# Reordering TensorE work inside the steps of the RWKV stage: side pieces before the projections instead of between two halves of them

## The chip, the cores and the metric

The kernel runs on one core of a Trainium2 chip. The metric is the device time of one execution in microseconds (us), as a median of several runs. One profiled execution gives the trace that is read here.

## The reference, cut to what matters

One decoder layer with two head groups of 8 heads x 64 over 1024 tokens of width 1024, all in float32. The normalised input goes through one wide input projection. Group A is sparse attention. Group B is the RWKV-7 recurrence, whose state depends on the token before:

```
h = rms_norm(x);  proj = h @ w_in          # columns for both groups
state, sa = 0, ...
for t in tokens:                            # per head, 64 x 64 state
    sa    = state @ (-kk_t)
    state = state * w_t + sa (x) (kk_t * a_t) + v_t (x) k_t
    y_t   = state @ r_t
y = group_norm(y) * gn_w + gn_b + bonus
out = rms_norm(x + concat(attention, y * gate) @ w_out)
```

## The kernel before, in words

The recurrence is computed in chunks of 64 tokens. The 1024 tokens x 8 heads are cut into 8 units (n = 0 to 7): a unit is two pairs of heads over 256 tokens, that is 4 chunks. Inside a chunk the recurrence is a triangular system, so a unit needs preparation (its **side work**) and then a **chain** of 12 dependent steps, three for each chunk (`wkv_chain`). A chain step is a burst of 8 small float32 matmuls in two groups into the PSUM tiles `pc` and `py`, and a copy of the result by VectorE (`z`, or `x1` at L682 and L689) and ScalarE (L683, L690). The next step's burst reads those copies.

`weave(n, ...)` runs the 12 steps of unit n. After each burst it puts other TensorE work, so that TensorE has something to do while the copies are made:

- **projections** (`filler.step`): matmuls of the input projection, 128x128 by 128x512 in fp32r, into tiles `p_...`, 48 to a group of 128 columns. Each step takes a quota of 7 or 8 of them (7 for n = 0, 1, 2, 6, 7; 8 for n = 3, 4, 5). The weights of the next group are fetched by DMA and split in two parts by ScalarE and VectorE (L342, L344) at fixed places within the group before (tiles `gn2r`, `gn2h`, `gn2l`, for example).
- **side pieces** (`piece(gen)`): generators that prepare later units or finish earlier ones. `sides` says at which of the 12 steps j each yields its next piece:
  - `wkv_values(n+1)`: transposes `pbt` (j = 0) and `pvt` (j = 1)
  - `wkv_elementwise(n+2)`: `pss` (first piece, at j = 11 of the unit before), `pw` (j = 1), `pa_` (2), `pn` (3), VectorE, ScalarE and GpSimd work at 4 and 5 (GpSimd L514, L522; VectorE L525), `pbon` (8)
  - `wkv_products(n+2)`: `pp` (j = 6 and 7), masked copies `g` (L555), then a DMA round trip `g` -> `dA` -> `la`, and from j = 10 through j = 5 of the next unit 31 rounds of two dependent GpSimd operations (L584, L586), which invert the triangles; the result goes through `dT` to `tt`
  - `wkv_inverse(n+1)`: VectorE transpose of `tt` (L633, j = 9), `px` (10), `pt` (11)
  - `wkv_norm(n-1)`: `pvar` (0), VectorE (2), `pyn` (4)
  - for n = 6 and 7 also `rotate` and `compress` (tiles `pcm`, weights `w`).

TensorE and GpSimd execute in the order in which the program is written (`manual_schedule(engines={PE, Pool})`). For VectorE, ScalarE and SyncE (which issues all DMAs, L85) a scheduler orders the instructions when the kernel is built: the chain has the highest priority, then the side pieces, then the projections' own copies and splits. `piece` adds that a side piece's VectorE and ScalarE instructions queue behind the chain's last copy on their engine (`gate`, `issue_after`); that is an order of issue, not a wait for completion.

A step of 12 that has no side piece on TensorE (j = 5 and 9, mostly) runs its whole quota of projections in one go already.

Of the kernel before, what the change touches and what calls it, by code (L numbers as in the profile page):

```python
# [74 lines left out]
def trunk_kernel(ctx, tc, x, norm_g, w_in, cmp_pos_k, cmp_w1_k, cmp_w2_k, cmp_pos_v, cmp_w1_v,  # L75
# [1143 lines left out]
    def g_gn(r):  # L1219
# [6 lines left out]
    filler = Filler([groups[n] for n in  # L1226
                     ("wda k0 k1 r0 r1 v0 v1 r2 k2 r3 k3 v2 v3 kc0 kc1 ks kw q0 q1 q2 q3 "
                      "gn1 gn0 gn2 gn3 gr0 gr1 gr2 gr3").split()])
# [4 lines left out]
    def piece(gen):  # L1233
        with ExitStack() as s_:
            s_.enter_context(tc.high_priority(offset=100000))
            for ins in gate.values():
                s_.enter_context(tc.issue_after(ins.ins))
            return next(gen, None)

    def whole(gen):  # L1240
        with tc.high_priority(offset=100000):
            for _ in gen:
                pass

    def weave(n, sides, quota):


        chain = wkv_chain(n)
        for j in range(12):
            with tc.high_priority(offset=200000):  # L1250
                next(chain)
            filler.step(quota // 2)
            for gen in sides.get(j, ()):
                piece(gen)
            filler.step(quota - quota // 2)
        whole(chain)

    TRI, EDGE, TRI_T, EDGE_T = range(4)
# [44 lines left out]
    with tc.manual_schedule(engines={E.PE, E.Pool}):  # L1303
# [7 lines left out]
        for n in range(8):  # L1311
# [43 lines left out]
            if n == 7:  # L1355
                nxt(1, 0, 1, 2, 3, 4, 5)
                side(call(lambda: begin(compress(1, cmp_w1_v, cmp_w2_v))), 3)
                nxt(2, 6, 7, 8, 9, 10, 11)
            weave(n, sides, (7, 7, 7, 8, 8, 8, 7, 7)[n])
        for g in keys:  # L1360
            assert next(g, None) is None
# [177 lines left out]
```

## Time and profile before

| what | value |
|---|---|
| three timed runs | 1038.44, 1043.26, 1045.9 us; median 1043.26 us |
| the profiled execution | 1040.26 us, of which the trace spans 1038.5 us |
| TensorE busy (matmuls) | 930.2 us, 90% of the span |
| VectorE, ScalarE, GpSimd busy | 584.0, 335.5, 448.2 us |
| mean granted TensorE clock | 0.951 of 2.4 GHz |
| the eight weaves (n = 0 to 7) | from 196.8 to about 581 us of the span |

PE is TensorE's matmuls, PEld its weight loads, DVE VectorE, ACT ScalarE, POOL GpSimd, SPq the queue on SyncE that issues DMAs. A matmul row's duration is modelled and overlaps the next; the distance from one start to the next is what TensorE really takes for it. "idle before <-X" is the time that the engine stood still ahead of an instruction, and what ended it.

### The profile page before, as it was taken

What the parts mean: (1) busy time and instruction counts of PE and PEld (TensorE: products, weight loads), DVE (VectorE), ACT (ScalarE), POOL (GpSimd) and SP (SyncE); (2) the same over time, 40 slices, a digit from 0 to 9 for tenths busy, and PEclk for the clock granted to TensorE, in tenths of its full rate; (3) what the DMA queues carried; (4) which work ended last, traced back from release to release, by engine and by line L of the source; (5) the groups of instructions that cost most, each with busy time, mean ns of one, the idle gap of its engine ahead of it and who ended that gap; (6) DMA issues with size and microseconds to landing.
All of it is one profiled execution on the core that took longest, in us unless ns stands there. A gap on an engine that the chain in (4) does not pass through costs nothing.

```text
span 1038.5 us, 17087 instructions
## 1 busy us (share of the span) xinstructions
PE 930.2 (90%) x6353; PEld 658.6 (63%) x6353; DVE 584.0 (56%) x1245; ACT 335.5 (32%) x650; POOL 448.2 (43%) x732
## 2 busy tenths in 40 slices
PE   5999999989998999899669978689999999889976
PEld 4888777766676766677458756354565656455555
DVE  7533545555575657374424335677659856685544
ACT  5533233224233443243121212433333333224321
POOL 3100153466483847444521120577463555246521
PEclk9999999999999999799889988879999999899989
DMA  7433453424426453536476293741132312231121
GB/s 259 125 102 102 125 157 108 130 76 116 135 76 172 134 154 119 131 106 170 116 218 192 65 203 95 212 122 31 41 63 79 77 46 69 53 80 33 39 84 41
DMA packets 154429, 115.66 MB, mean 111 GB/s; under 512 B 54369, under 2 KB 132266, under 8 KB 154346
## 3 DMA queue, kind: packets, MB, share of 16 engines
q1 hardware_dynamic: 154346, 114.57, 40.3%
q8 instruction: 50, 0.82, 0.3%
q14 instruction: 33, 0.27, 0.1%
HBM read 76.19 MB, written 35.19 MB: 107 GB/s over the span
## 4 chain that ended last, share of the span: by engine, by line
PE 60%; DVE 10%; DMA 9%; POOL 7%; SPq 6%; issue 5%; ACT 2%; POOLq 0%; DVEq 0%; ACTq 0%
PE pout L113 7%; SPq L85 6%; PE pst L113 6%; PE po L113 5%; PE p_r L113 4%; PE p_k L113 3%; PE p_gn L113 3%; PE p_gr L113 3%; PE p_q L113 3%; PE pc L113 2%; POOL lt L586 2%; POOL ltmp L584 2%; PE ps L113 2%; PE pd L113 2%; PE pcm L113 2%
## 5 line engine op out<-in xcount | busy, mean ns | idle before, releaser
L584 POOL TENSOR_TENSOR ltmp<-la,lt 128x60 f32<-128x60 f32 (+24 forms) x248 | 83.7, 337 | 65.3 <-DMA la<-dA 42.7
L1042 ACT ACTIVATE prob<-pst 128x512 f32<-128x512 f32 x132 | 74.6, 593 | 109.9 <-PE pst L113 106.3
L1055 POOL TENSOR_TENSOR acc<-acc,prob 128x1024 f32<-128x1024 f32 x36 | 86.7, 2409 | 45.1 <-ACT prob L1042 44.9
L586 POOL TENSOR_TENSOR lt<-lt,ltmp 128x60 f32<-128x60 f32 (+24 forms) x248 | 87.6, 353 | 18.8
L113 PE MATMUL pst<-q,k 128*128 128x512 f32 (+1 forms) x264 | 82.3, 430 | 0.0
L994 DVE TENSOR_REDUCE bm<-ps 128x6 f32<-128x384 f32 (+1 forms) x106 | 63.5, 613 | 26.6 <-PE ps L113 26.0
L113 PE MATMUL po<-prob,vt 128*64 128x512 f32 x264 | 75.1, 648 | 0.0
L1055 POOL TENSOR_TENSOR acc<-prob 128x1024 f32<-128x1024 f32 x14 | 33.7, 2410 | 82.6 <-ACT prob L1042 82.6
L113 PEld LDWEIGHTS pst<-q,k 128*128 128x128 f32 (+1 forms) x264 | 48.9, 196 | 14.9 <-issue 5.7
L113 PE MATMUL pout<-woh,mh 128*128 128x512 f32 x128 | 57.6, 450 | 0.2 <-DVE xt L1153 0.2
L113 PE MATMUL ps<-k,q 128*128 128x384 f32 (+3 forms) x136 | 45.4, 386 | 7.7 <-DVE bm L994 3.7
L113 PE MATMUL pout<-wol,mh 128*128 128x512 f32 x128 | 51.3, 401 | 0.0
L113 PE MATMUL pout<-woh,ml 128*128 128x512 f32 x128 | 51.2, 400 | 0.0
L113 PEld LDWEIGHTS ps<-k,q 128*128 128x128 f32 x136 | 25.6, 205 | 35.2 <-DVE bm L994 14.3
L982 DVE TENSOR_REDUCE bm<-pd 128x8 f32<-128x512 f32 x40 | 27.4, 688 | 26.2 <-PE pd L113 26.0
L113 PEld LDWEIGHTS pout<-woh,mh 128*128 128x128 f32 x128 | 25.1, 196 | 20.7 <-issue 17.8
L683 ACT ACTIVATE x<-pc 64x128 f32<-64x128 f32 x32 | 8.7, 272 | 75.4 <-DVE x L682 75.2
L113 PE MATMUL pd<-k,q 128*128 128x128 f32 x160 | 31.1, 321 | 2.1 <-POOL k L868 2.1
L1077 POOL TENSOR_TENSOR wide<-rr,ones 128x512 f32<-128x512 f32 x16 | 17.1, 1068 | 36.1 <-DVE rr L1073 34.1
L1069 DVE TENSOR_REDUCE zz<-pz 128x4 f32<-128x512 f32 x32 | 21.8, 684 | 13.4 <-PE pz L1067 13.0
L1153 DVE TENSOR_TENSOR xt<-pout,xt 128x512 f32<-128x512 f32 x16 | 11.1, 691 | 32.4 <-PE pout L113 32.4
L113 PEld LDWEIGHTS pd<-k,q 128*128 128x128 f32 x160 | 25.9, 204 | 4.0 <-POOL k L868 2.4
(518 smaller groups left out, 2447.7 us busy)
## 6 DMA issues: line engine op xcount, KB each, us to landing
dM<-mix SPq DMA_DIRECT2D x24, 256.0 KB
q<-dQH SPq DMA_DIRECT2D x22, 256.0 KB
la<-dA SPq DMA_DIRECT2D x32, 128.0 KB
xt<-in_x_dram SPq DMA_DIRECT2D x8, 512.0 KB
out_dram<-xt SPq DMA_DIRECT2D x16, 256.0 KB
x<-in_x_dram SPq DMA_DIRECT2D x7, 512.0 KB
mixk<-dM SPq DMA_DIRECT2D x8, 256.0 KB
mixr<-dM SPq DMA_DIRECT2D x8, 256.0 KB
```

Source lines behind the costliest of these rows:

```text
L85: return nc.sync.dma_start(plain(o), plain(i))
L113: return T.matmul(o, l, r, start=start, stop=stop)
L584: G.tensor_tensor(tv, la[:, j:j + 1, j + 1:].to_broadcast([128, m, n]), lt[:, :m, j:j + 1].to_broadcast([128, m, n]), op=OP.mult)
L586: G.tensor_tensor(lt[:, :m, j + 1:], lt[:, :m, j + 1:], tv, op=OP.add)
L683: gate["A"] = A.activation(x1[1][HP[1], c:8:4, :], pv[HP[1], :, 64:128], AF.Copy)
L982: V.tensor_reduce(bm[:, g * 4:g * 4 + 4, j:j + 2], p.rearrange("p (r b c) -> p r b c", b=2, c=64), axis=AX.X, op=OP.max)
L994: V.tensor_reduce(bm[:, h0:h0 + n, j:j + 2 * w], p[:, :n * w * 128].rearrange("p (h b c) -> p h b c", h=n, c=64), axis=AX.X, op=OP.max)
L1042: A.activation(pr[:, g * 512:(g + 1) * 512], p, AF.Exp)
L1055: G.tensor_tensor(s, self.acc, pr, op=OP.add)
L1069: V.tensor_reduce(zz[:, g, :], p.rearrange("p (r k) -> p r k", r=4), axis=AX.X, op=OP.add)
L1077: G.tensor_tensor(wide, rr.rearrange("p r g -> p (r g)").unsqueeze(2).to_broadcast([128, 8, 64]), ones64.unsqueeze(1).to_broadcast([128, 8 ...
L1153: V.tensor_tensor(xt[:, hs], p, xt[:, hs], op=OP.add)
```

## The change

Within a step, the first half of the quota of projections moves from before the side pieces to behind them, so that all of a step's projections follow each other. The number of projections in a step, the side pieces and their steps stay as they are.

```diff
@@ -1249,10 +1249,9 @@
         for j in range(12):
             with tc.high_priority(offset=200000):
                 next(chain)
-            filler.step(quota // 2)
             for gen in sides.get(j, ()):
                 piece(gen)
-            filler.step(quota - quota // 2)
+            filler.step(quota)
         whole(chain)
```

## Rows read from the trace of the kernel before

**Rows 1.** Busy time by engine in unit n = 1, 3, 6 (stretch, length, busy, PEclk).

```profile
241.70:287.20 45.50, 43.16 (x457) 30.95 (x456) 25.82 (x66) 15.16 (x34) 27.92 (x73) 0.98 0.42 113
334.30:380.80 46.50, 45.49 (x453) 32.83 (x452) 28.05 (x69) 18.02 (x38) 28.12 (x69) 0.99 0.54 155
480.80:527.60 46.80, 37.80 (x401) 27.05 (x400) 22.52 (x42) 12.94 (x27) 30.97 (x63) 0.89 0.49 138
```

**Rows 2.** Timeline of PE, unit 1, steps 4 and 5 (start, duration, instruction).

```profile
259.01 0.50 PE L113 MATMUL p_kc<-hl,kc0h 128*128 128x512 f32 x1
...
259.81 0.60 PE L720 MATMUL pyn<-ident,nq 128*128 128x128 f32 x4
260.16 0.48 PE L113 MATMUL p_kc<-hl,kc0h 128*128 128x512 f32 x1
...
261.27 0.45 PE L113 MATMUL pc<-x,bt 128*64 128x64 f32 x8
...
261.88 0.50 PE L113 MATMUL p_kc<-hh,kc0h 128*128 128x512 f32 x1
...
263.70 0.45 PE L113 MATMUL pc<-x,g 128*64 128x64 f32 x8
```

**Rows 3.** Timeline of PE, unit 2, step 7: the three projections ahead of `pp`.

```profile
313.68 0.50 PE L113 MATMUL p_ks<-hl,ksh 128*128 128x512 f32 x1
...
314.58 1.16 PE L113 MATMUL pp<-ar,bk 64*128 64x128 f32 x16
```

**Rows 4.** Waits of PE from 196.8 to 581 us (total us, times, longest).

```profile
PE pcm L113 <- DMA w<-in_cmp_w_k_dram: 8.0, 1, 8.0
PE pss L113 <- ACT s L467: 5.9, 4, 2.1
PE p_gn L113 <- DVE gn2l L344: 4.9, 1, 4.9
PE p_gn L113 <- ACT gn2h L342: 4.1, 1, 4.1
PE pc L113 <- ACT x L683: 3.6, 2, 3.2
PE pp L113 <- DVE bk L525: 3.0, 4, 1.0
PE px L113 <- DVE t L633: 1.4, 3, 0.6
```

**Rows 5.** Timeline of all engines, unit 1, step 11.

```profile
281.78 0.40 PE L113 MATMUL py<-g,x 128*64 128x64 f32 x8
...
282.23 0.60 ACT L697 ACTIVATE nq<-py 128x512 f32<-128x512 f32 x1 [0.97 <-PE py L113]
...
283.88 0.90 ACT L467 ACTIVATE s<-mixk,cols 128x256 f32<-128x256 f32 x2
...
284.44 1.05 PE L113 MATMUL pss<-mi,s 128*128 128x2 f32 x8 [1.36 <-ACT s L467]
```

**Rows 6.** Timeline from 284.9 to 331.7 us: one turn of the triangles' rounds (POOL, SP, DVE, PE).

```profile
284.93 0.24 POOL L584 TENSOR_TENSOR ltmp<-la,lt 128x31 f32<-128x31 f32 x1 [5.50 <-DMA dKC<-kca]
...
308.56 1.46 POOL L522 TENSOR_TENSOR s<-s,mixk 128x512 f32<-128x512 f32 x1
...
310.05 0.75 DVE L525 TENSOR_TENSOR bk<-s,s 128x512 f32<-128x512 f32 x1 [1.17 <-POOL s L522]
...
310.85 1.16 PE L113 MATMUL pp<-ar,bk 64*128 64x128 f32 x16 [0.63 <-DVE bk L525]
...
315.54 2.56 SPq L85 DMA_DIRECT2D dT<-lt  x4
...
326.69 2.15 SPq L85 DMA_DIRECT2D la<-dA  x4
...
331.69 0.24 POOL L584 TENSOR_TENSOR ltmp<-la,lt 128x31 f32<-128x31 f32 x1 [7.83 <-DMA la<-dA]
```

**Rows 7.** Busy time and PEclk around a wait of unit 2's last step.

```profile
328.70:332.10 3.40, 1.47 (x38) 1.45 (x40) 0.48 (x3) 1.90 (x5) 0.33 (x2) 1.00 0.84 232
332.20:335.50 3.30, 3.30 (x28) 2.19 (x21) 1.27 (x5) 0.00 (x0) 2.52 (x11) 0.50 0.93 304
```

**Rows 8.** Timeline of DVE, then PE, unit 4, step 10, and PEclk behind it.

```profile
424.56 0.69 DVE L344 TENSOR_TENSOR q3l<-q3r,q3h 128x512 fp32r<-128x512 f32 x1 [5.05 <-ACT q3h L342]
425.17 0.28 DVE L682 COPY x<-pc 64x128 f32<-64x128 f32 x1
...
425.86 0.69 PE L113 MATMUL pc<-x,bt 128*64 128x64 f32 x8 [3.17 <-ACT x L683]
...
424.40:437.90 13.50, 10.92 (x84) 8.14 (x84) 4.72 (x18) 4.88 (x12) 9.04 (x29) 0.50 0.61 165
```

## Prediction

> **What bounds the kernel now.** I read the busy time by unit first, then the timeline of TensorE step by step, then its waits, and last the timeline of the engine that ends the recurring wait.
>
> By unit, TensorE is nearly full where no long wait falls: 43.16 of 45.50 us in unit 1 and 45.49 of 46.50 in unit 3, against 28 us for VectorE and for GpSimd [rows 1]. So a reader would expect a saving on TensorE to shorten the stage. The waits correct this. Most of TensorE's idle time is in a few long waits for DMA-fed data (`pcm` 8.0 us, `gn2l` and `gn2h` 4.9 and 4.1, `x` 3.2), and the recurring ones are two: `pss` for ScalarE, 5.9 us in 4 times, and `pp` for L525, 3.0 us in 4 times [rows 4]. The second is the important one, for what stands behind it is a loop that hardly contains TensorE. GpSimd begins the 31 rounds at 284.93 us when `la` has landed, works without a gap to L522 at 308.56, VectorE's L525 follows at 310.05 and `pp` starts at 310.85, having waited; the rounds' result leaves as `dT` at 315.54, `tt` and `dA` follow it in SyncE's queue, `la` is issued at 326.69 and lands for the next L584 at 331.69 [rows 6]. That turn takes 46.76 us, as long as the unit (287.2 to 334.3). `pp` showed such a wait in units 0, 1, 2 and 4 (4 times in rows 4). So as far as unit 4's step 6, at about 406 us, the stage goes by GpSimd and the DMA round trip, with TensorE close behind; from there to 581 us by TensorE and the long waits.
>
> **What the change removes.** One break in the run of projections. Three projections ahead of `pyn` take 0.80 us (259.01 to 259.81) and the four behind it 1.11 (260.16 to 261.27), 1.91 together; seven in one run take 1.82 (261.88 to 263.70) [rows 2]. So a step whose first side piece is a full-height one like `pyn` saves 0.09 us. Ahead of a half-height piece the three take 0.90 (313.68 to 314.58) [rows 3], and such a step saves 0.90 + 1.11 - 1.82 = 0.19 us. By the timeline 74 of the 96 steps carry a side piece on TensorE: 35 begin with a half-height one (`pbt` 7, `pvt` 7, `pp` 12, `px` 7, `pt` 2), 39 with a full-height one (`pyn` 7, `pa_` 6, `pbon` 6, `pss` 5, `pn` 5, `pcm` 8, `pw` 1, `pvar` 1). What a side piece costs directly behind the burst the trace shows too rarely to price; its first weight load may wait there for the burst, as it does not behind projections in the full-height case. I take 0 to 0.09 us saved in those 39, and 0.19 in the 35: 6.7 to 10.2 us of TensorE's time over the stage.
>
> The Trainium skill (TensorE: Matmul & The Clock Gate, Part 2, on loading the stationary operand) says that TensorE pulls weight loads ahead of matmuls still running. Taken alone that would make a break free and the saving zero; rows 2 and 3 show 0.09 and 0.19 us, and the measurement decides.
>
> **What the change adds.** The three or four projections that stood between burst and side piece were cover. Any side piece whose input comes later than the burst's end now bares that much more idle time: 0.80 to 0.90 us with a quota of 7, about 1.1 with 8 (four at the pitch of rows 2).
>
> - `pss` (units 0 to 4, step 11). The burst's last group starts at 281.78; ScalarE then does L697, the copy, L699 and L467, from 282.23 to past 284.4, and `pss` starts at 284.44 after 1.36 us of idle time [rows 5]. ScalarE's work does not move, since it follows the burst, so `pss` starts at the same distance and the idle time grows by 0.80. Three times 0.80 in units 0 to 2, 1.1 in unit 4, 0 to 1.1 in unit 3, where it did not wait: 3.5 to 4.6 us.
> - The first `pp` (units 0 to 5). Where it waited already it waits 0.9 longer (three times) or 1.1 (unit 4); 0 to 1.1 in units 3 and 5: 3.8 to 6.0 us.
> - `pcm` once, for its weights: 0.8. `px` once or more: 0.6 was its longest wait, 0.9 more.
> - The pieces that follow one another from step to step (`pbt` to `pvt`, `pw` to `pa_`, `px` to `pt`, `pp` to `pp`) shift together, so their distance stays a step: nothing.
>
> Together 9.0 to 12.3 us bared, against 6.7 to 10.2 saved. **If TensorE bound everything**, that would be -1.2 to +5.6 us. Behind a waiting side piece stand the projections and the next burst, in TensorE's own order; nobody else waits for them soon, as the chain's copies are then long made.
>
> **Where it falls.** Up to 406 us neither counts much. The loop of rows 6 holds TensorE in one step, between the two `pp` pieces, which come 0.2 us closer; and `dA` stands in SyncE's queue behind `tt`, which waits for GpSimd and not for `pp`. So `pp` of units 0 to 4 starts where it did, give or take: 0, with bounds of -1 (0.2 five times) and +2 (a DMA issued ahead of `la`). GpSimd's order is unchanged, since projections have almost no GpSimd work.
>
> From there on TensorE counts again:
>
> - unit 4, step 6: `pp` at the same time, but eight projections behind it instead of four: +0.9
> - steps left with a break removed: 12 half-height (2, 6 and 4 in units 4, 5, 6) at -0.19, so -2.3; some 17 full-height at -0.09 to 0, I take -0.05, so -0.8
> - bared: `pss` of unit 4 +1.1, `pp` of unit 5 +1.0 (L525 ended just ahead of it), `pcm` +0.8, so +2.9
>
> Sum: +0.7 us. The attention stage, from 581 us, is as before. The profiled execution took 1040.3 us, so 1041 by its account; the median of the runs lies 3.0 above it, and I forecast on that basis: 1043.3 + 0.7 = **1044 us**, no measurable change. About 1% (10.4 us) is what a measurement of this kernel can tell from none.
>
> **The rivals.**
>
> *Longer idle times cost clock (slower).* The rows show it once plainly: between 328.70 and 332.10 TensorE was busy 1.47 of 3.40 us at the full granted clock, 2.4 GHz, and in the next 3.30 us the grant was 0.50, that is 1.2 GHz [rows 7]. With half the rate, 3.3 us at that level lose some 1.6. The change makes five waits at `pss` (to 2.2 us and more) and four to six at `pp` (to about 1.6) longer. If each of some nine of them brings such a stretch, that is 15 us; GpSimd's loop hides part in units 0 to 3, though TensorE's slack there is only the idle time at `pp`. With the +0.7 and 60 to 90% of the 15 uncovered it gives 1053 to 1058 us; it decides from six such stretches in all. Against it: `pss` waited 1.36 us in unit 1 and the clock of that unit was 0.98 all the same [rows 1, 5]. The skill's page on TensorE (Part 1, the clock gate) states the same rule, that idle time lowers the clock and that gaps should be avoided; it speaks against this change. The trace agrees in rows 7.
>
> *The saving comes through and queues sort themselves out (faster).* In unit 4 the chain's copy L682 stood on VectorE behind a weight split that waited for its DMA; TensorE waited 3.17 us and then ran at 0.50 for 13.5 us, which lost about half of that [rows 8]. With side work out of VectorE's way earlier in each step, or with another order from the scheduler, this could vanish: -3.2 - 6.7, with 6.7 to 10.2 saved and only half of the bared time: about -13, 1030 us. Against it: the wait is for a fetch, which the change does not move ahead.
>
> *Another order on SyncE, VectorE and ScalarE.* The scheduler lays these queues out anew. The waits for `gn2` (9.0 us) and `w` (8.0) hang on the place of one DMA among others [rows 4]; either may shrink or grow by several us, of either sign. This widens the forecast's own range to 1036 to 1052.
>
> **How the numbers follow.** Forecast 0.66; clock and bared waits 0.20; saving and queues 0.14. The likeliest gives 1044. To leave out no more than 2 in 10 the range takes in part of both others: 1034 to 1056. Faster by over 1% (under 1032.8) 0.12, slower by over 1% (above 1053.7) 0.20, within 0.68.
>
> **What would show it.** Right: runs of seven take 1.82 us everywhere; `pss` idles 2.1 us or more in units 0 to 2 and `pp` 1.5; GpSimd's first L584 of each unit comes at the old distance (44 to 48 us). Wrong: GpSimd's turn shortens by more than 1 us, or idles for `pp`; PEclk of units 0 to 4 falls under 0.9; or one of the waits for `gn2`, `w` or `q3` changes by over 5 us, which would swamp the rest.

## The result, and the profile after

| | before | after |
|---|---|---|
| median of 6 runs each on one chip | 1042.72 us (1038.44 to 1045.9) | 1053.13 us (1051.47 to 1059.15) |
| span of the profiled execution | 1038.5 us | 1050.3 us |
| mean granted TensorE clock | 0.951 | 0.940 |

The ratio is 1.0106 [1.0072, 1.0141]: slower, by 10.4 us, on the border of what the prediction set as measurable (1%). The time lies within its range and 9 us above its point. The ratios, here and below, leave out executions over 1.5% slower than the fastest of their kernel and weigh all the others, so they can differ from the quotient of the medians by some 0.15%.

The first window of [rows 1], with unit 0 ahead of it (units 0 and 1 of the changed kernel: length, then busy us of PE, PEld, DVE, ACT, POOL, then PEclk, DMA share, GB/s):

```profile
154.70:248.40 93.70, 84.17 (x716) 64.33 (x715) 45.63 (x91) 26.37 (x55) 44.87 (x124) 0.96 0.41 109
248.40:295.40 47.00, 42.50 (x436) 31.74 (x434) 28.21 (x68) 15.65 (x35) 29.30 (x74) 0.94 0.40 112
```

Waits of PE in the changed kernel, as [rows 4] (total us, times, longest):

```profile
PE pss L113 <- ACT s L467: 10.5, 5, 3.4
PE pcm L113 <- DMA w<-in_cmp_w_k_dram: 9.4, 1, 9.4
PE pp L113 <- DVE bk L525: 7.8, 5, 4.2
PE p_gn L113 <- ACT gn2h L342: 4.7, 1, 4.7
PE p_gn L113 <- DVE gn2l L344: 3.9, 1, 3.9
```

In total the bared waits came as forecast: `pss` +4.6 us, `pp` +4.8, `pcm` +1.4; the waits for `gn2` stayed within 1 us of before. But they don't say where the time went. For that the trace is cut at fixed instructions: VectorE's first copy `z` of each unit, and the first matmul into `pst`, with which the attention stage begins. Both kernels were profiled a second time, for one execution alone shows what recurs no better than what doesn't. All are differences of start times in the traces, in us:

| | up to unit 0 | unit 0 | units 1 to 6 | unit 7 to first `pst` | from `pst` to the end | span |
|---|---|---|---|---|---|---|
| before | 153.5 | 89.0 | 285.7 | 92.7 | 417.6 | 1038.5 |
| before, again | 156.8 | 88.9 | 288.3 | 95.3 | 418.4 | 1047.6 |
| after | 154.7 | 93.7 | 287.5 | 92.5 | 421.8 | 1050.3 |
| after, again | 157.0 | 93.1 | 288.3 | 90.5 | 423.7 | 1052.6 |

By the means of the pairs: unit 0 +4.4 us, units 1 to 6 +0.9, unit 7 and behind -2.5, attention +4.8, start +0.7; together the 8.4 by which the mean spans differ (1051.45 and 1043.05). Only unit 0 and the attention stand clear of the scatter between two executions of one kernel. The stage as a whole, from the first `z` to the first `pst`, does not: 467.4 and 472.5 us before, 473.8 and 471.8 after. The change reorders the steps of unit 0 as of every unit; in the attention stage it touches not a line.

**Unit 0.** First SyncE's queue before, then that of the changed kernel, where `lc` are the masks for the attention and `v3r` is a weight fetch that waits for its buffer:

```profile
194.87 1.18 SPq L85 DMA_DIRECT2D lc<-in_late_dram  x2
...
199.01 0.38 SPq L85 DMA_DIRECT2D v3r<-in_w_in_dram  x1
```

```profile
199.87 0.38 SPq L85 DMA_DIRECT2D v3r<-in_w_in_dram  x1
200.30 1.34 SPq L85 DMA_DIRECT2D lc<-in_late_dram  x2
```

The scheduler put `lc` behind `v3r`; counted from the unit's first `z` it is issued 4.2 us later (200.30 - 154.7 against 194.87 - 153.5). GpSimd's order in unit 0 changed too. The rounds that run there and the casts of the masks (L1272; L1273 before) are written ahead of the `manual_schedule` block, and there GpSimd does not keep the program's order, other than the section on the kernel before has it. In the traces of before the two casts stand behind 6 begun rounds, L514 behind 14 and L522 behind 22; in both traces of after the casts stand behind 8 and 9, L514 behind 13 and L522 behind 20. From unit 1 on both kernels have L514 behind 20 and L522 behind 24. GpSimd in unit 0, first before, then after (the round behind L522 is the 23rd, of 54 columns, or the 21st, of 66):

```profile
195.90 0.24 POOL L584 TENSOR_TENSOR ltmp<-la,lt 128x31 f32<-128x31 f32 x1 [5.72 <-DMA la<-dA]
...
217.18 1.28 POOL L522 TENSOR_TENSOR s<-s,mixk 128x512 f32<-128x512 f32 x1
...
218.54 0.79 POOL L584 TENSOR_TENSOR ltmp<-la,lt 128x54 f32<-128x54 f32 x1
...
240.29 0.24 POOL L584 TENSOR_TENSOR ltmp<-la,lt 128x31 f32<-128x31 f32 x1 [6.35 <-DMA la<-dA]
```

```profile
196.83 0.24 POOL L584 TENSOR_TENSOR ltmp<-la,lt 128x31 f32<-128x31 f32 x1 [5.46 <-DMA la<-dA]
...
204.68 0.61 POOL L1272 CAST maskb<-lc 128x512 bf16<-128x512 f32 x1 [2.13 <-DMA lc<-in_late_dram]
...
219.37 1.26 POOL L522 TENSOR_TENSOR s<-s,mixk 128x512 f32<-128x512 f32 x1
...
220.71 0.80 POOL L584 TENSOR_TENSOR ltmp<-la,lt 128x66 f32<-128x66 f32 x1
...
244.36 0.24 POOL L584 TENSOR_TENSOR ltmp<-la,lt 128x31 f32<-128x31 f32 x1 [8.01 <-DMA la<-dA]
```

TensorE of the changed kernel:

```profile
216.75 0.45 PE L113 MATMUL py<-ar,x 64*64 64x64 f32 x8
221.40 2.08 PE L113 MATMUL pp<-ar,bk 64*128 64x128 f32 x16 [4.21 <-DVE bk L525]
...
225.76 0.45 PE L113 MATMUL pc<-z,tt 64*64 64x64 f32 x8
```

The same step before, and then the windows behind `pp` (PEclk is the third number from the end), before, after and in the second profile of after:

```profile
217.27 0.45 PE L113 MATMUL py<-ar,x 64*64 64x64 f32 x8
...
219.24 1.16 PE L113 MATMUL pp<-ar,bk 64*128 64x128 f32 x16 [0.62 <-DVE bk L525]
...
221.45 0.45 PE L113 MATMUL pc<-z,tt 64*64 64x64 f32 x8
```

```profile
219.20:221.40 2.20, 2.16 (x20) 1.64 (x20) 2.20 (x5) 0.24 (x1) 1.81 (x6) 1.00 0.49 137
```

```profile
221.30:225.70 4.40, 4.30 (x23) 3.46 (x23) 2.23 (x5) 0.22 (x1) 3.47 (x12) 0.62 0.58 179
```

```profile
223.90:228.30 4.40, 4.40 (x22) 3.69 (x23) 2.13 (x4) 0.00 (x0) 3.46 (x13) 0.50 0.58 179
```

From the unit's first `z`, TensorE reaches this burst 1.7 us earlier than before (216.75 - 154.7 against 217.27 - 153.5): the saving of the steps ahead is real. But GpSimd stands 2.13 us for `lc`, and L522 comes 1.0 us later, though two rounds fewer stand ahead of it; L525 ends later and `pp` starts 1.0 us later, so TensorE stands for 4.21 us instead of 0.62. Behind that wait it runs near 1.2 GHz: `pp` and its seven projections take 4.36 us where `pp` and four took 2.21, and three projections in a long run are worth 0.8 (three of seven in 1.81), so by this estimate 1.4 us are the clock's. GpSimd's turn is 47.5 us (45.8 in the second profile), before 44.4 and 44.3.

**The attention.** VectorE in its second tile, first before, then after:

```profile
698.00 0.19 DVE L930 SCALAR_TENSOR_TENSOR im<-imh,im 128x32 f32<-128x32 f32 x1
698.23 0.20 DVE L931 TENSOR_TENSOR im<-im,keep 128x32 f32<-128x32 f32 x1
...
700.37 0.69 DVE L1093 TENSOR_TENSOR t<-t,pos 128x512 f32<-128x512 f32 x1
```

```profile
706.21 0.94 DVE L930 SCALAR_TENSOR_TENSOR im<-imh,im 128x32 f32<-128x32 f32 x1
707.18 2.29 DVE L931 TENSOR_TENSOR im<-im,keep 128x32 f32<-128x32 f32 x1
...
711.42 2.22 DVE L1093 TENSOR_TENSOR t<-t,pos 128x512 f32<-128x512 f32 x1
```

GpSimd beside them, first before, then after:

```profile
695.10 2.80 POOL L1114 TENSOR_TENSOR wol<-wor,woh 128x1024 fp32r<-128x1024 f32 x1
700.51 2.79 POOL L1055 TENSOR_TENSOR acc<-acc,prob 128x1024 f32<-128x1024 f32 x1 [2.61 <-ACT prob L1042]
```

```profile
706.06 1.04 POOL L1077 TENSOR_TENSOR wide<-rr,ones 128x512 f32<-128x512 f32 x1
707.06 2.37 POOL L1114 TENSOR_TENSOR wol<-wor,woh 128x1024 fp32r<-128x1024 f32 x1
710.75 2.34 POOL L1055 TENSOR_TENSOR acc<-acc,prob 128x1024 f32<-128x1024 f32 x1 [1.32 <-ACT prob L1042]
```

Before, all three small operations begin in a gap of GpSimd (697.90 to 700.51). After, each begins while a GpSimd operation runs, and the first two end when those end (707.15 and 707.10; 709.47 and 709.43). They take 5.45 us instead of 1.08. `bm` (L994), for which TensorE waits, stands behind them on VectorE. Here the order on GpSimd is the scheduler's, and it put a weight split (`wol`) elsewhere.

All of the stage's loss can be seen to arise here: from this L930 to the next L1009 on VectorE it is 9.2 us in both traces of before and 14.1 in both of after, and from there to the third tile's L930 81.7 in all four; by the means the stretch ahead is 1.2 us longer and the one behind 1.4 shorter. The 4.9 us are not simply the three operations' 4.4, for two later ones, L1095 and L1126, take 1.94 and 1.91 us before and 0.69 and 0.68 after. TensorE shows the rest: in the changed kernel it stands for `bm`, and from 714.9 to 720.0 us PEclk is 0.67 (1.00 from 701.6 to 706.8 before). The wait, and then all waits of TensorE for `bm` L994 in this stage, before and after:

```profile
714.89 0.44 PE L113 MATMUL ps<-k,q 128*128 128x384 f32 x1 [2.02 <-DVE bm L994]
```

```profile
PE ps L113 <- DVE bm L994: 3.7, 7, 0.9
```

```profile
PE ps L113 <- DVE bm L994: 6.7, 8, 2.0
```

### The profile page after: what moved, and what is told of

The parts are those of the page before. It is cut to its first block, busy times and chain, and to the rows that moved or that the text cites. A ratio compares the mean times of both kernels' runs of the same rounds, so it can differ in the third digit from the quotient of the medians.

```text
span 1050.3 us, 17094 instructions
## 1 busy us (share of the span) xinstructions
PE 926.2 (88%) x6353; PEld 664.6 (63%) x6353; DVE 586.9 (56%) x1245; ACT 333.9 (32%) x650; POOL 445.0 (42%) x732
## 4 chain that ended last, share of the span: by engine, by line
PE 57%; DMA 12%; DVE 11%; issue 6%; POOL 6%; SPq 5%; ACT 2%; POOLq 0%; DVEq 0%; ACTq 0%
PE pout L113 7%; PE pst L113 6%; PE po L113 5%; SPq L85 5%; PE p_r L113 4%; PE p_k L113 3%; PE p_gr L113 3%; PE p_q L113 3%; PE pc L113 2%; PE ps L113 2%; PE p_kc L113 2%; PE pcm L113 2%; POOL ltmp L584 2%; PE pd L113 2%; PE pp L113 2%
## 5 line engine op out<-in xcount | busy, mean ns | idle before, releaser
L584 POOL TENSOR_TENSOR ltmp<-la,lt 128x60 f32<-128x60 f32 (+24 forms) x248 | 87.6, 353 | 59.1 <-DMA la<-dA 25.7
L586 POOL TENSOR_TENSOR lt<-lt,ltmp 128x60 f32<-128x60 f32 (+24 forms) x248 | 82.3, 332 | 18.9
L994 DVE TENSOR_REDUCE bm<-ps 128x6 f32<-128x384 f32 (+1 forms) x106 | 63.6, 613 | 27.6 <-PE ps L113 27.0
L113 PE MATMUL ps<-k,q 128*128 128x384 f32 (+3 forms) x136 | 45.8, 386 | 11.5 <-DVE bm L994 6.7
L1069 DVE TENSOR_REDUCE zz<-pz 128x4 f32<-128x512 f32 x32 | 21.8, 684 | 13.4 <-PE pz L1067 13.1
```

Of the source, the lines that this page charges most:

```text
L113: return T.matmul(o, l, r, start=start, stop=stop)
L584: G.tensor_tensor(tv, la[:, j:j + 1, j + 1:].to_broadcast([128, m, n]), lt[:, :m, j:j + 1].to_broadcast([128, m, n]), op=OP.mult)
L586: G.tensor_tensor(lt[:, :m, j + 1:], lt[:, :m, j + 1:], tv, op=OP.add)
L994: V.tensor_reduce(bm[:, h0:h0 + n, j:j + 2 * w], p[:, :n * w * 128].rearrange("p (h b c) -> p h b c", h=n, c=64), axis=AX.X, op=OP.max)
L1069: V.tensor_reduce(zz[:, g, :], p.rearrange("p (r k) -> p r k", r=4), axis=AX.X, op=OP.add)
```

## The experiments

Three theories stood against each other. A: the stage goes by GpSimd's rounds and their DMA trip, and the change lengthened that loop. B: the waits that the change bared on TensorE (`pss`, `pp`) cost the time themselves. C: a change in the order of program lays the scheduled queues out anew, anywhere, and that is what it costs. The text set off in each case was written before the run; "before" is the kernel before, run beside it.

| kernel | median us (runs) | before, beside it | ratio |
|---|---|---|---|
| masks early | 1059.14 (6) | 1045.38 (17) | 1.0132 [1.0086, 1.0178] |
| cover at steps 6, 11 | 1057.92 (6) | same | 1.0106 [1.0056, 1.0157] |
| unit 0 alone | 1056.12 (6) | same | 1.0113 [1.007, 1.0156] |
| units 5 to 7 alone | 1051.26 (12) | same | 1.0051 [1.0016, 1.0085] |
| before, 16 rounds | 1043.72 (12) | 1046.33 (35) | 0.9977 [0.9948, 1.0006] |
| after, 16 rounds | 1042.66 (12) | same | 0.9973 [0.9944, 1.0001] |
| masks' place fixed | 1053.07 (12) | same | 1.0071 [1.0037, 1.0106] |
| halves swapped | 1052.93 (12) | same | 1.0059 [1.0027, 1.009] |
| before, L522 on VectorE | 1047.2 (12) | 1046.68 (23) | 1.0017 [0.999, 1.0044] |
| masks' place fixed, L522 on VectorE | 1052.36 (12) | same | 1.0069 [1.0037, 1.0101] |

**The masks fetched earlier**, in the changed kernel, so that `lc` is long there when GpSimd casts it:

```diff
     filler.through("k2")
+    load_masks()
...
     filler.through("k3")
-    load_masks()
```

> The changed kernel with one thing moved: the masks (DMA lc, two GpSimd casts) are loaded ahead of unit 1's products instead of just ahead of the weaves, so that GpSimd cannot wait for them inside unit 0. Theory A (the stage goes by the GpSimd and DMA loop, and the loss comes in where that loop was lengthened: 2.1 us of GpSimd idle for lc in unit 0): 2 to 3 us under the changed kernel, 1050 to 1051 us. Theory B (the bared waits of pss and pp on TensorE are the loss): no difference, 1053 us.

1.0132. The wait for `lc` is gone, but SyncE's order moved with it: GpSimd's rounds began at 203.5 us, behind a DMA wait of 10.0, and unit 0 took 96.8 us. The edit replaced one accident of the queues by a larger one and doesn't price the first.

**Cover given back at the two waiting pieces**, in the changed kernel: half the quota stands ahead of the side pieces again at steps 6 and 11.

```diff
-            for gen in sides.get(j, ()):
-                piece(gen)
-            filler.step(quota)
+            first = 0 if j not in (6, 11) else quota // 2
+            filler.step(first)
+            for gen in sides.get(j, ()):
+                piece(gen)
+            filler.step(quota - first)
```

> The changed kernel, but steps 6 and 11, where pp and pss waited, keep the old order with half of the projections ahead of the side pieces. Theory A: what those waits take is given back by GpSimd's loop in units 0 to 3, so at most 3 us under the changed kernel, 1050 to 1053 us. Theory B: pss and pp had 9 us more idle time in the changed kernel, so it returns to the kernel before or under it, 1039 to 1045 us.

The waits went back to the size of [rows 4]; TensorE's waits of this kernel, 150 to 600 us:

```profile
PE pss L113 <- ACT s L467: 6.7, 4, 2.6
PE pp L113 <- DVE bk L525: 2.4, 2, 1.9
```

The time did not: 1.0106. So the loss doesn't go with these waits. That alone does not rule B out, for this edit, like the one before, laid the queues out anew: unit 0 (91.6 us) and the attention (420.8) stayed long, and units 1 to 6 took 295.9 us, 7.6 more than the longer of the two traces of after.

**The change in unit 0 alone**, then **in units 5 to 7 alone** (same lines, with `first = 0 if n == 0 else quota // 2`, and with `n >= 5`):

> The new order in unit 0 alone, the old one in units 1 to 7. Theory A: unit 0 is where the loop got longer (its turn 47.5 instead of 44.4 us), so 3 to 4 us over the kernel before, 1046 to 1047 us. Theory B: one of five pss waits and one of six pp waits, less the saving in ten steps: 0 to 1.5 us over the kernel before, 1043 to 1044 us.

> The new order in units 5, 6 and 7 alone. From the first pp of unit 5 to the end of the stage the changed kernel fell 3 us further behind. Theory A (there TensorE and the DMA waits set the time, and the changed order of the queues costs): 2 to 4 us over the kernel before, 1045 to 1047 us. Theory B: no pss and one pp lie there, with some 20 steps saved: 1041 to 1043 us.

Unit 0 alone costs as much as the whole change (1.0113), and its profile has both marks: unit 0 at 92.3 us, the attention at 421.9. Units 5 to 7 alone leave unit 0 as it was (88.5 us) and still cost 0.5%, with the attention at 420.8 us: that much of a loss needs no change ahead of unit 5.

**GpSimd's rounds cut from 31 to 16** in the kernel before and in the changed one. The rest of the inverse is left out.

```diff
-        for j in range(31):
+        for j in range(16):
```

> The kernel before with 16 instead of 31 of GpSimd's rounds in each unit (the rest of the inverse is left out, so the output is not the reference's). GpSimd's turn falls from 44 to 48 us to about 37. Theory A (GpSimd and DMA loop, TensorE close behind): pp stops waiting and the stage goes by TensorE, 3 to 6 us under the kernel before, 1039 to 1042 us. Theory B (bared waits on TensorE alone): the same within 2 us, since pp's inputs are VectorE's.

> The changed kernel with 16 instead of 31 rounds (output not the reference's). Theory A: the lengthened loop no longer counts, what is left is TensorE's own account of the change, -1 to +6 us against the same cut of the kernel before: 1040 to 1047 us. Theory B: pss and pp stay bared, 10 us over the same cut of the kernel before. Theory C (each change of the program's order lays the queues of SyncE, VectorE and ScalarE out anew, and that costs, wherever TensorE's order changed): 5 to 12 us over it, with the loss in places of no one kind.

Now the change costs nothing: 1043.72 and 1042.66 us. GpSimd's waits in the changed kernel with 16 rounds, 190 to 600 us, show that its loop ends nothing there, for it waits for the others:

```profile
POOL bk L563 <- PE pp L113: 45.1, 6, 12.0
```

Both kernels with 16 rounds have the long stretch in the attention (14.1 us from L930 to L1009), so here it doesn't part them. TensorE's own account of the change, bared waits and all, is then about even. But A is not thereby shown. Halving the rounds buys the kernel before only 2.6 us, not clear of the noise, and its units 0 to 3 take 225.5 us instead of 227.8 and 232.1 in the two traces of before: as far as these tell, the loop binds there with TensorE 0.6 to 1.6 us a unit behind it. And unit 0 of the changed kernel still takes 92.8 us with 16 rounds (86.4 before), with `pp` waiting 4.8 us; the other stretches make up for it.

**The masks' place fixed**, in the changed kernel: the projections of a step queue behind the masks' DMA, so that `v3r` can't pass it.

```diff
+    masks_in = []
...
-            dma(lc, late[:, src:src + 512])
+            masks_in.append(dma(lc, late[:, src:src + 512]))
...
-            filler.step(quota)
+            with tc.issue_after(masks_in[-1].ins):
+                filler.step(quota)
```

> The changed kernel with one order on SyncE restored: the first fetch of v3's weights is queued behind the masks' DMA lc, as it stood in the kernel before. GpSimd then does not wait for lc in unit 0 (2.1 us). Theory A: 2 us under the changed kernel, 1051 us beside 1053. Theory B: no difference. Theory C: 2 us at most, and the rest of the loss stays.

SyncE of this kernel, unit 0:

```profile
198.87 1.11 SPq L85 DMA_DIRECT2D lc<-in_late_dram  x2
...
204.12 0.94 SPq L85 DMA_DIRECT2D v3r<-in_w_in_dram  x1
```

GpSimd no longer waits for `lc`; `pp` waits for 4.7 us in all instead of 7.8, unit 0 takes 91.3 us instead of 93.7 and 93.1. The total (1.0071) can't be told from the changed kernel's, and the attention, at 423.9 us, carries its mark still. The profile parts unit 0's loss in two. Counted from the unit's first `z`, `pss` at step 11 starts at 84.8 us, as before (84.8 and 84.4; 87.6 and 88.0 in the changed kernel): up to there nothing of the loss is left, though GpSimd's order is still that of the changed kernel (8, 9, 13, 20). From `pss` to the next unit's first `z` it takes 6.5 us (4.2 and 4.5 before, 6.1 and 5.1 after): three more projections stand there, worth 0.8, and PEclk is 0.54 (0.70 and 0.64 before, over these stretches).

**The halves swapped**, in the kernel before: `quota - quota // 2` projections ahead of the side pieces, `quota // 2` behind. With a quota of 7 one projection changes sides, with 8 none.

```diff
-            filler.step(quota // 2)
+            filler.step(quota - quota // 2)
             for gen in sides.get(j, ()):
                 piece(gen)
-            filler.step(quota - quota // 2)
+            filler.step(quota // 2)
```

> The kernel before with its two parts swapped where they differ: in the units with a quota of 7, four projections ahead of the side pieces and three behind. One projection (0.23 us) more cover for pss and pp. Theory B: the waits shrink by 0.23 us in about six places, so 0 to 2 us under the kernel before. Theory C: this harmless change lays the queues out anew as well and costs 3 to 10 us. Theory A: the same as before within 2 us.

This costs 0.6% (1.0059), with more cover, not less, ahead of the waiting pieces. It is the run that speaks most plainly for C. Its loss lies elsewhere again: unit 0 (88.9 us), the attention (417.5) and GpSimd's order in unit 0 are as before, units 1 and 6 take 50.0 and 51.2 us. Unit 6 is longer for an order on SyncE: TensorE waits 13.1 us for `gn2h` and `gn2l` together, 9.0 and 9.2 us in the two traces of before. SyncE issues the first two `gn2r` at 482.28, as in the second trace of before (482.27). Then the scheduler put one `gn2r` ahead of the eight transfers `ropa` and `ropw`; SyncE stands 5.0 us for L344 before it, all of these wait behind it, and the last `gn2r` leaves at 507.42 instead of 503.18 (the second of the two in the last row). SyncE with the halves swapped, then before, again:

```profile
493.07 0.39 SPq L85 DMA_DIRECT2D gn2r<-in_w_in_dram  x1
...
507.42 0.38 SPq L85 DMA_DIRECT2D gn2r<-in_w_in_dram  x1
```

```profile
487.90 0.68 SPq L85 DMA_DIRECT2D ropa<-dQ  x1
...
501.99 1.56 SPq L85 DMA_DIRECT2D gn2r<-in_w_in_dram  x2
```

**Both kernels again**, for one profile each:

> The kernel before once more, for a second trace: how far the start (first chain copy at 153.5 us), the stage (467.3 us from there to the attention's first scores) and the attention behind it (417.6 us) vary from one execution to another. No theory parts here; Theory A and B take unit 0's 89.0 us as that kernel's own, so 88 to 90 us again.

> The changed kernel once more, for a second trace. Theory A and Theory B: unit 0 again 93 to 95 us from first copy to first copy, the stage 472 to 476 us. Theory C: the same. If unit 0 comes back to 89 to 90 us, its loss was one execution's.

1049.36 and 1054.36 us; they are the second and fourth line of the table of stretches. Within one kernel single units differ by up to 3.5 us between executions (unit 1 before: 45.9 and 49.4), so the units of one profile carry no cause by themselves. Unit 0, GpSimd's order in it and the small operations of the attention did recur.

**L522 moved from GpSimd to VectorE**, in the kernel before and in the changed one with the masks' place fixed. L525, and with it `pp`, then no longer waits until GpSimd's rounds have come to L522, as in [rows 6].

```diff
-        G.tensor_tensor(th, th, k, op=OP.mult)
+        V.tensor_tensor(th, th, k, op=OP.mult)
```

> The kernel before with one operation of the loop (L522, 1.28 us on GpSimd, just ahead of the first pp) moved to VectorE. Theory A: pp waits less (3.0 us in all before) and GpSimd's turn is 1.3 us shorter; 2 to 5 us under the kernel before. Theory B: no change within 1 us. Theory C: a new laying out of the queues, so 3 to 10 us over it in spite of the shorter loop.

> The changed kernel with v3's fetch queued behind the masks' DMA and L522 on VectorE. Theory A: GpSimd's turn is shorter and no longer waits for the masks, so 4 to 7 us under the changed kernel and no slower than the kernel before by more than 3 us. Theory B: pss stays bared, 2 us at most under the changed kernel. Theory C: no order of the queues is known in advance, within 5 us of the changed kernel.

1.0017 and 1.0069: no gain in either. But they don't settle what a shorter loop is worth, for GpSimd's turn did not get shorter: 44.7, 45.3, 48.8 and 51.3 us from unit 0 on with L522 moved in the kernel before, 44.4, 44.6, 46.8 and 46.8, or 44.3, 48.4, 46.7 and 47.3, in the two traces without. None of the versions with all 31 rounds beats the kernel before.

**The attention over all 14 profiles.** No edit was made in its code, but the three VectorE operations of its second tile (L930, L931, L1093) fall into three classes, by how much longer than before's 1.08 us they take together:

| extra on VectorE | L930 to L1009, us | kernels | `pst` to the end, us | mean |
|---|---|---|---|---|
| 0 | 9.2 | before twice, halves swapped | 417.6, 418.4, 417.5 | 417.8 |
| 2.1 | 11.2 to 11.9 | L522 moved, twice; cover at 6, 11 | 417.5, 418.9, 420.8 | 419.1 |
| 3.7 to 4.4 | 14.1 to 14.3 | after twice; masks early; masks fixed; unit 0; units 5 to 7; 16 rounds, twice | 419.4 to 424.9 | 422.2 |

From that L1009 to the third tile's L930 it is 80.4 to 81.7 us in all 14, so the classes part in these few microseconds and hardly behind them. Before with 16 rounds is in the last class too (419.4), with the old order of projections: no change in TensorE's program order is needed for it, other durations upstream are enough. This is a correlation over kernels; the order on GpSimd itself was not pinned, so it was not tried whether that brings the stage back.

## Why the prediction was right or wrong

The size class and TensorE's account are right as far as the runs tell; the place of the loss is wrong. That the time lies in the range is luck: the range went up to 1056 us to take in part of the rivals, the likeliest value was 1044, and the loss arose in two places that the sum put at nothing.

- **The break in the run**: right. Seven projections in unit 2 now take 1.81 us (forecast 1.82), and ahead of them a full-height piece saves next to nothing, as its lower bound had it: `pa_` directly behind the burst takes 1.25 us. PE timeline of the changed kernel, unit 2:

```profile
304.45 1.31 PE L113 MATMUL pa__3301<-aS,up 128*128 128x256 f32 x4
305.70 0.49 PE L113 MATMUL p_kc<-hh,kc1h 128*128 128x512 f32 x1
...
307.51 0.45 PE L113 MATMUL pc<-x,g 128*64 128x64 f32 x8
```

- **The bared waits**: right for `pss`, which idles 2.25 us in units 0 and 1 and 2.28 in unit 2 (forecast 2.1 or more); +4.6 in all against 3.5 to 4.6. For `pp` the total is right by luck: +4.8 against 3.8 to 6.0, but 3.6 of it is the one wait in unit 0. In units 1 to 4 `pp` waits 1.37, 0.69, 0.98 and 0.58 us (before 0.97, 0.63, 0 and 0.76), +1.3 where 0.9 to 1.1 was forecast for each of three and up to 1.1 for the fourth: counted from its unit's first `z`, `pp` itself started 0.7 to 1.6 us earlier there. `pcm` +1.4 against 0.8. Set against the saving they come out about even, if the kernels with 16 rounds tell it rightly. The row in unit 1, to compare with [rows 5]:

```profile
286.33 0.40 PE L113 MATMUL py<-g,x 128*64 128x64 f32 x8
288.99 1.44 PE L113 MATMUL pss<-mi,s 128*128 128x2 f32 x8 [2.25 <-ACT s L467]
```

- **"Up to 406 us 0, with bounds of -1 and +2"**: from the first `z` to the first `pp` of unit 4 it was +4.2 us in the first pair of traces and +0.5 in the second; what recurs is unit 0, +4.7 and +4.2. The step that failed is "GpSimd's order is unchanged", from which "`pp` starts where it did" was drawn. In unit 0 the order was the scheduler's and did change (L522 behind 20 rounds, not 22), and GpSimd waits in it for a DMA whose place on SyncE is the scheduler's too: 2.1 us for `lc`. The two `pp` pieces, which were to come 0.2 us closer, are 1.25 us further apart there (226.38 - 221.40 against 222.97 - 219.24), for the clock fell between them. From unit 1 on the order is unchanged, and the turns of the loop (45.0, 46.9, 46.5 us; before 44.6, 46.8, 46.8) bear the step out. (The first row of [rows 6] names `dKC`, not `la`, as what ended that wait; the trace has `la` issued right ahead of it, at 279.90 to 281.20 us.)
- **From unit 4, step 6, to 581 us, +0.7**: borne out, as far as the scatter allows. From that `pp` to the first `pst` it was +2.2 in the first pair and -1.2 in the second.
- **"The attention stage is as before"**: wrong, +4.8 us, and the largest single miss. It was put at nothing without a reason: that its source doesn't change was taken for its order not changing, but GpSimd's and VectorE's orders are the scheduler's there.
- **The rivals.** The clock: it happened, behind `pp` in unit 0 (0.62 and 0.50; 1.00 before), behind `pss` in unit 1 (0.57 and 0.53; 1.00 and 0.86 before) and, over 4 us, behind `pss` in unit 3 (0.88 and 0.74; 1.00 twice before): three stretches where the rival decided from six. From the first `z` to the first `pst` PEclk was 0.92 and 0.93, before 0.95 and 0.93. The stretch in unit 1, in the changed kernel, then in the kernel before, 3.3 us from the start of `pss`:

```profile
289.00:292.30 3.30, 3.30 (x42) 3.10 (x43) 0.98 (x3) 0.33 (x1) 2.28 (x10) 0.57 0.34 67
```

```profile
284.40:287.70 3.30, 3.26 (x56) 2.69 (x58) 1.23 (x4) 1.27 (x3) 2.14 (x9) 1.00 0.45 82
```

  The time came close to its 1053 to 1058 us, but most of it not by it: the clock had a share in unit 0 and in the attention, behind waits that other queue orders had made. The saving coming through: units 1 to 7 show little of it. Queues laid out anew: this was the rival that came true, with the size of its upper end, but not at the waits that were named for it (`gn2`, `w`); its places were unit 0, with the masks, and the attention.

What stays open: whether the order on GpSimd alone makes the attention's 4.9 us, since no run pinned it, and what in the change moves that order. Of unit 0's 4.4 us the masks' place is worth some 3 by the starts of `pss`, the rest arises behind `pss`; one trace with the masks fixed says so.

## What to carry to other kernels

Where a scheduler orders some queues, count the change's cost in stages that it doesn't touch as well: here 4.8 of 8.4 us arose in the attention, some 80 us behind its first matmul. That an engine keeps the order of the program is to be read from the trace, stretch by stretch: GpSimd kept it from unit 1 on, not in unit 0. And a fixed order is only as fixed as the DMAs that it waits for. Before a difference of under 1% is put down to a reason, move one instruction that can't matter (here one projection per step, 0.6%) and profile both kernels twice.

## What the runs showed of the hardware

Small VectorE operations stretched while GpSimd ran beside them: in the rows of the attention 128x32 took 0.19 and 0.20 us in a gap of GpSimd, 0.94 and 2.29 beside a GpSimd operation, and 128x512 (L1093) 0.69 and 2.22. The Trainium skill (GPSIMD Engine Reference, 1. Specifications) says that GpSimd shares its SBUF interfaces with VectorE and contends with VectorE instructions that have two SBUF inputs; the rows agree, and those that end within 0.05 us of the GpSimd operation look like waiting for it rather than sharing.

A wait was not always followed by the lower clock: behind `pss` in unit 1, after the same wait of 1.36 us, PEclk was 1.00 in one execution of the kernel before and 0.86 in the other; after 2.25 us it was 0.57 and 0.53 in the two of the changed kernel. And a low PEclk behind a wait need not come from that wait: behind `pss` in unit 4 before (430.10, a wait of 1.1 us) it is 0.50, but it was 0.50 already from 424.3 on, as [rows 8] show.

Two executions of one kernel differ by 3 us before the first unit begins (153.5 and 156.8) and by up to 3.5 us in one unit.
